# A convolution's norm and Silu ordered ahead of the third head's attention, with the rows of the output projection behind the attention

## The chip, the cores and the metric

The kernel runs on one core of a Trainium2 chip. The metric is the device time of one execution in microseconds (us). A core has TensorE (PE, matmuls; PEld is its weight load), VectorE (DVE), ScalarE (ACT), GpSimd (POOL) and SyncE (SP), which here only issues DMAs. Each engine works its own list of instructions in the order in which they were put down, and waits for others by semaphores.

## The reference

One layer of a streaming encoder, for 512 frames of a new stream and 32 frames of a running one (the sample):

```
mod = silu(c) @ w_ada + b_ada               # shift, scale and gate, twice
h   = x * (1 + sc1) + sh1
z   = h @ w_in + b_in                       # conv value | conv gate | q | k | v
u   = conv_a * sigmoid(conv_b)              # 512 channels
dw  = causal depthwise conv(u), width 31
conv_out = silu(layer_norm(dw))             # norm over the 512 channels
q, k = rope(q), rope(k)                     # 4 heads, two maps of 64 each
p   = softmax of both maps, block-causal in chunks of 64
att = rms_norm((p0 - lam * p1) @ v) * subln_g * (1 - lam_init)    # per head
x   = layer_norm(alpha * x + g1 * (concat(conv_out, att) @ w_out + b_out))
x   = layer_norm(alpha * x + g2 * peer(x * (1 + sc2) + sh2))
```

The last step (peer) selects 16 of 128 x 128 experts for each of 8 heads of a frame and takes up most of the time.

## The kernel before

The program is written with a library that puts the instructions of each engine in order itself: it plays the program on a timing model and sets down, engine by engine, whatever is ready and stands earliest in the text. So the order of the text gives priorities, and the pools of buffers decide what can be ready. The order that comes out is fixed for the chip.

The part that matters here runs from about 145 to 300 us. Eight projection units (`zunit`, two for each head, key then query, 48 matmuls each, line 191) make the keys and queries of a head in two banks of the pool `pa` (function `pat`, two banks in all). ACT adds the bias (line 438), SP swaps halves of 32 rows by four small DMAs (`zw`, line 440), and DVE does the rotation (lines 442 to 445). Then come four attention maps of 128 rows for each head: two score matmuls into a pair of banks (`big`, line 461), maximum on DVE (334), two exponentials on ACT (345), reciprocals, on ACT the first map times its reciprocal (358), on DVE the difference of the two maps (361, into `a`), transposes on PE (467), a copy to `aT` (469), the product with the values (472) and the head's sum of squares and copy on ACT (367, 368). The attention of the sample (`sample_att`) takes all four heads in one map and stands in the text after the fourth head's projection.

The convolution is 124 instructions on DVE, the taps (lines 270 and 273, into `acc`), kept in order by the chain in `conv_taps` and called a few at a time beside the projections and maps (`conv(CB)`, `conv(CZ)`). At the place that `CN` names, the text calls for the rest of them and for `conv_norm`: means by a matmul with ones into two banks of `pa` (376), differences on DVE (379), squares on ACT (383), variances again into two banks of `pa` (385, taken out at 388), root on ACT (389), reciprocal and scaling on DVE (390, 392). With `CN = (3, -1)` that is ahead of the fourth head's attention.

Behind the heads, the Silu of the convolution goes to a buffer `mt` (490, 491), which is split in two parts of reduced precision, `mixh` and `mixl` (492, 493). The heads' outputs are scaled, transposed and split likewise (498 to 510). The output projection (`wgroup`, line 582) multiplies both with the split weights `woh` and `wol` (576, 578), first for tiles 3 and 4, then for tiles 0, 1 and 2. Its rows are prepared by `xload`: b_out times the gate into `bg` (550), and the input rows times alpha plus `bg` (560). Behind it come the query projection and the selection of experts, and then, from about 500 us to the end, the dense products with the expert tables.

Of the kernel before, what the change touches and what calls it, by code (L numbers as in the profile page):

```python
# [8 lines left out]
F32 = mybir.dt.float32  # L9
# [11 lines left out]
NP = 512  # L21
NS = 32
# [38 lines left out]
EXTRA = 8  # L61
RUN = 2
LAST = 4
CN = (3, -1)
CB = 4
CZ = 2
QW = (6, 10, 13)
# [9 lines left out]
def build(tc, I, O):  # L77
# [250 lines left out]
    V.tensor_sub(neglam, lsum[:, 1:2], lsum[:, 0:1])  # L328
    V.tensor_scalar(neglam, neglam, -LAM0, None, op0=OP.add)

    def softmax_parts(parts, ex):
        mx = at.tile([128, 2, 2], F32, tag="mx", name="mx")
        for n, p in enumerate(parts):
            V.tensor_reduce(mx[:, n, :], p, axis=AX.X, op=OP.max)
        nm = at.tile([128, 2], F32, tag="nm", name="nm")
        src = mx[:, 0, :]
        if len(parts) == 2:
            m2 = at.tile([128, 2], F32, tag="m2", name="m2")
            V.tensor_max(m2, mx[:, 0, :], mx[:, 1, :])
            src = m2  # L340
        V.tensor_scalar(nm, src, -0.125, None, op0=OP.mult)
        se = at.tile([128, 2, 2], F32, tag="se", name="se")
        for n, p in enumerate(parts):
            for m in range(2):
                S.activation(ex[n][:, m], p[:, m], AF.Exp, bias=nm[:, m:m + 1], scale=0.125,
                             accum_out=se[:, n, m:m + 1])
        ss = se[:, 0, :]
        if len(parts) == 2:
            s2 = at.tile([128, 2], F32, tag="s2", name="s2")
            V.tensor_add(s2, se[:, 0, :], se[:, 1, :])  # L350
            ss = s2
        rc = at.tile([128, 2], F32, tag="rc", name="rc")
        V.reciprocal(rc, ss)
        rl = at.tile([128, 1], F32, tag="rl", name="rl")
        V.tensor_mul(rl, rc[:, 1:2], neglam)
        out = []
        for n, e in enumerate(ex):
            S.activation(e[:, 0], e[:, 0], AF.Copy, scale=rc[:, 0:1])
            w = e.shape[2]
            a = at.tile([128, 512 if n == 0 else NS], F32, tag=f"a{n}", name="a")  # L360
            V.scalar_tensor_tensor(a[:, :w], e[:, 1], rl, e[:, 0], op0=OP.mult, op1=OP.add)
            out.append(a)
        return out

    def head_out(po, i, h, r):
        sq = at.tile([128, 128], F32, tag="sq", name="sq")
        S.activation(sq[:r], po, AF.Square, accum_out=oms[:r, i, h:h + 1])
        S.copy(otok[:r, i, h, :], po)

    HC = CO // 2  # L370

    def conv_norm():
# [17 lines left out]
        V.reciprocal(crs, crs)  # L390
        for c in range(4):
            V.tensor_mul(acc[:, c], acc[:, c], crs.rearrange("p a b -> p (a b)"))

    pT = [slice(0, 64), slice(64, 128)]
    def sample_att():
# [12 lines left out]
                          tile_position=(64 * m, 32 * h))  # L408
        e = at.tile([128, 2, 512], F32, tag="e", name="e")
        en = at.tile([128, 2, 32], F32, tag="en", name="en", bufs=1)  # L410
        a, an = softmax_parts([sc, sn[:, :, :NS]], [e, en])
        pt = sm()
        for kb in range(4):
            PE.transpose(pt[:, kb * 128:(kb + 1) * 128], a[:, kb * 128:(kb + 1) * 128], ident)
# [14 lines left out]
    for h in range(4):  # L429
# [27 lines left out]
        for i in ((0, 1, 2, 3) if h < 3 else (3, 0, 1, 2)):  # L457
            kl = 128 * (i + 1)
            sc = big()
            for m in range(2):  # L460
                PE.matmul(sc[:, m, :kl], qh[pT[m], i * 128:(i + 1) * 128], kh[pT[m], :kl], start=True, stop=True)
            V.memset(sc[:64, :, kl - 64:kl], NEG)
            e = at.tile([128, 2, 512], F32, tag="e", name="e")
            a, = softmax_parts([sc[:, :, :kl]], [e[:, :, :kl]])
            pt = sm()
            for kb in range(i + 1):
                PE.transpose(pt[:, kb * 128:(kb + 1) * 128], a[:, kb * 128:(kb + 1) * 128], ident)
            aT = at.tile([128, 512], F32, tag="aT", name="aT")
            (V.tensor_copy if h >= 3 else S.copy)(aT[:, :kl], pt[:, :kl])
            po = sm() if h < 3 else pat()  # L470
            for kb in range(i + 1):
                PE.matmul(po[:, :128], aT[:, kb * 128:(kb + 1) * 128], vt[:, kb, h * 128:(h + 1) * 128],
                          start=(kb == 0), stop=(kb == i))
            head_out(po[:, :128], i, h, 128)
            conv(CB)
            if (h, i) == CN:
                conv(124)
                conv_norm()
# [7 lines left out]
    mixh = mixp.tile([128, KC, TM], F32R, name="mixh", bufs=1)  # L486
    mixl = mixp.tile([128, KC, TM], F32R, name="mixl", bufs=1)
    for c in range(4):
        mt = mixp.tile([128, TM], F32, tag="mt", name="mt")
        S.activation(mt[:, :NP], acc[:, c, :NP], AF.Silu, bias=lnb[:, c:c + 1], scale=lng[:, c:c + 1])  # L490
        S.activation(mt[:, NP:], acc[:, c, NP + 30:CO], AF.Silu, bias=lnb[:, c:c + 1], scale=lng[:, c:c + 1])
        V.tensor_copy(mixh[:, c, :], mt)
        V.tensor_sub(mixl[:, c, :], mt, mixh[:, c, :].bitcast(F32))
    for i in (4, 3, 0, 1, 2):
        r = ROWS[i]
        if i in (4, 0):
# [50 lines left out]
    bg = []  # L547
    for s in range(2):
        t = op_.tile([128, D], F32, tag="row", name="bg", bufs=4) if s == 0 else xhB[0]
        V.tensor_mul(t, bo, g1r[s])  # L550
        bg.append(t)
    g1w = rowload(I["ln1_g"])
    b1w = rowload(I["ln1_b"])
# [2 lines left out]
    def xload(i):  # L556
        t = op_.tile([128, D], F32, tag="xp", name="xp", bufs=3) if i < TA else xhB[i - TA]
        r = ROWS[i]
        SY.dma_start(t[:r], I["xtok"][i * 128:i * 128 + r])
        V.scalar_tensor_tensor(t[:r], t[:r], ALPHA, bg[i // 4][:r], op0=OP.mult, op1=OP.add)  # L560
        xps[i] = t

    xload(4)
# [579 lines left out]
```

## Time and profile before

| | us |
|---|---|
| timed runs, median of 3 (lowest to highest) | 1649.08 (1644.37 to 1650.94) |
| the profiled execution | 1638.17 |
| its span, first to last instruction | 1636.4 |
| PE busy | 1567.4 (96%) |
| DVE busy | 1390.4 (85%) |
| ACT busy | 619.1 (38%) |
| POOL busy | 468.4 (29%) |

The times in the rows count from the start of the span. A busy share is an average over stages that differ much, so the rows below are of the stage of the change. The granted clock is the share of full speed at which PE was allowed to run: 1.00 is 2.4 GHz, 0.50 is 1.2 GHz. An idle time in brackets stands ahead of the instruction and names what ended it.

### The profile page before, as it was taken

What the parts mean: (1) busy time and instruction counts of PE and PEld (TensorE: products, weight loads), DVE (VectorE), ACT (ScalarE), POOL (GpSimd) and SP (SyncE); (2) the same over time, 40 slices, a digit from 0 to 9 for tenths busy, and PEclk for the clock granted to TensorE, in tenths of its full rate; (3) what the DMA queues carried; (4) which work ended last, traced back from release to release, by engine and by line L of the source; (5) the groups of instructions that cost most, each with busy time, mean ns of one, the idle gap of its engine ahead of it and who ended that gap; (6) DMA issues with size and microseconds to landing.
All of it is one profiled execution on the core that took longest, in us unless ns stands there. A gap on an engine that the chain in (4) does not pass through costs nothing.

```text
span 1636.4 us, 24735 instructions
## 1 busy us (share of the span) xinstructions
PE 1567.4 (96%) x8911; PEld 1354.1 (83%) x8911; DVE 1390.4 (85%) x2674; ACT 619.1 (38%) x1073; POOL 468.4 (29%) x325
## 2 busy tenths in 40 slices
PE   7999987999988999999999899999999999999996
PEld 4878855786668999999999798888888888888884
DVE  3879987789999999999898668888778778788997
ACT  3312567333122443444454333333333333333332
POOL 0000000000144445247424123533334333244530
PEclk9999987999999999999999999999999999999998
DMA  9776342274478889999999998999999999999993
GB/s 345 286 233 214 86 145 95 77 233 141 140 253 278 293 274 328 342 343 335 367 358 366 372 316 310 347 356 341 352 337 342 328 347 346 336 319 331 338 322 108
DMA packets 184539, 465.59 MB, mean 285 GB/s; under 512 B 17537, under 2 KB 85185, under 8 KB 181217
## 3 DMA queue, kind: packets, MB, share of 16 engines
q1 hardware_dynamic: 138336, 296.23, 52.5%
q0 software_dynamic: 46080, 167.79, 28.9%
q8 instruction: 70, 1.15, 0.3%
q14 instruction: 53, 0.43, 0.1%
HBM read 415.57 MB, written 45.77 MB: 282 GB/s over the span
## 4 chain that ended last, share of the span: by engine, by line
PE 81%; DVE 8%; DMA 5%; issue 3%; ACT 3%; SPq 0%; POOL 0%; DVEq 0%; ACTq 0%
PE acc L994 32%; PE pat L911 30%; PE big L191 3%; PE pat L191 2%; PE pat L685 2%; PE big L826 2%; PE big L582 2%; DMA rowg<-in_u_ji_dram,idx 1%; PE pat L316 1%; PE pat L152 1%; DMA wr<-in_w_ada_dram 1%; DMA raw<-in_uT_dram 1%; DVE jkg L858 1%; DVE s L664 1%; DMA rt<-mod_d 1%
## 5 line engine op out<-in xcount | busy, mean ns | idle before, releaser
L847 POOL DMA_INDIRECT rowg<-in_u_ji_dram,idx x160 | 212.7, 1330 | 789.1 <-DVE VT L661 442.1
L902 DVE TENSOR_TENSOR lo<-raw,hi 128x1024 fp32r<-128x1024 f32 x256 | 311.8, 1220 | 107.4 <-ACT hi L900 101.2
L900 ACT CAST hi<-raw 128x1024 fp32r<-128x1024 f32 x256 | 266.8, 1047 | 307.4 <-PE acc L994 211.8
L847 POOL DMA_INDIRECT rowg<-in_vd_dram,idx x160 | 253.9, 1587 | 328.5 <-DVE accB L869 94.7
L994 PE MATMUL acc<-hi,Pl 128*128 128x512 f32 x768 | 300.8, 392 | 0.0
L994 PE MATMUL acc<-lo,Ph 128*128 128x512 f32 x768 | 281.2, 390 | 0.0
L994 PE MATMUL acc<-hi,Ph 128*128 128x512 f32 x768 | 245.1, 393 | 2.7 <-issue 2.7
L911 PE MATMUL pat<-h2h,hi 128*128 128x384 f32 x1024 | 212.9, 342 | 6.4 <-ACT hi L900 3.3
L911 PE MATMUL pat<-h2h,lo 128*128 128x384 f32 x1024 | 210.3, 342 | 4.8 <-DVE lo L902 4.8
L911 PE MATMUL pat<-h2l,hi 128*128 128x384 f32 x1024 | 210.0, 341 | 0.0
L858 DVE SCALAR_TENSOR_TENSOR jkg<-rowg,xhB 128x1024 f16<-128x1024 f32 x160 | 194.8, 1217 | 10.8 <-DMA rowg<-in_u_ji_dram,idx 8.6
L869 DVE SCALAR_TENSOR_TENSOR accB<-rowg,wB,accB 128x1024 f32<-128x1024 f32 x158 | 201.7, 1277 | 0.5
L911 PEld LDWEIGHTS pat<-h2h,hi 128*128 128x128 f32 x1024 | 181.7, 188 | 13.8 <-ACT hi L900 6.2
L911 PEld LDWEIGHTS pat<-h2h,lo 128*128 128x128 f32 x1024 | 182.2, 188 | 8.3 <-DVE lo L902 5.1
L911 PEld LDWEIGHTS pat<-h2l,hi 128*128 128x128 f32 x1024 | 184.0, 189 | 2.6
L994 PEld LDWEIGHTS acc<-hi,Ph 128*128 128x128 f32 x768 | 144.2, 188 | 30.3 <-issue 3.2
L994 PEld LDWEIGHTS acc<-lo,Ph 128*128 128x128 f32 x768 | 144.1, 188 | 29.1
L994 PEld LDWEIGHTS acc<-hi,Pl 128*128 128x128 f32 x768 | 144.7, 188 | 28.2
L917 ACT ACTIVATE ge<-pat 128x384 f32<-128x384 f32 x128 | 62.6, 491 | 193.5 <-PE pat L911 119.4
L980 ACT CAST Ph<-P 128x384 fp32r<-128x384 f32 x128 | 65.1, 511 | 144.3 <-issue 87.1
L982 DVE TENSOR_TENSOR Pl<-P,Ph 128x384 fp32r<-128x384 f32 x128 | 70.8, 553 | 35.6 <-ACT Ph L980 35.2
L273 DVE SCALAR_TENSOR_TENSOR acc<-U,wdw,acc 128x574 f32<-128x574 f32 x120 | 96.6, 805 | 1.4
(303 smaller groups left out, 1885.6 us busy)
## 6 DMA issues: line engine op xcount, KB each, us to landing
raw<-in_uT_dram SPq DMA_DIRECT2D x128, 512.0 KB
raw<-in_vd_dram SPq DMA_DIRECT2D x128, 512.0 KB
wr<-in_w_ada_dram SPq DMA_DIRECT2D x48, 512.0 KB
g_d<-stg SPq DMA_DIRECT2D x24, 1024.0 KB
gc<-g_d SPq DMA_DIRECT2D x16, 1536.0 KB
wq<-in_w_query_dram SPq DMA_DIRECT2D x32, 512.0 KB
ge_d<-ge SPq DMA_DIRECT2D x70, 192.0 KB
gel<-ge_d SPq DMA_DIRECT2D x70, 192.0 KB
```

Source lines behind the costliest of these rows:

```text
L191: PE.matmul(p[h], a[:, k * 128:(k + 1) * 128], b[:, k, h * HT:(h + 1) * HT], start=(q == 0 and k == 0), stop=(q == 2 and k == KC - 1))
L273: t = V.scalar_tensor_tensor(acc[:, c], U[:, c, w:w + CO], wdw[:, c, w:w + 1], acc[:, c], op0=OP.mult, op1=OP.add)
L847: g = G.indirect_dma_start(out=t, out_offset=None, in_=tab, in_offset=bass.IndirectOffsetOnAxis(ap=idx, axis=0))
L858: V.scalar_tensor_tensor(jk, t, 1.0, h2B[s], op0=OP.mult, op1=OP.mult, accum_out=aB[s][:, q:q + 1])
L869: V.scalar_tensor_tensor(ac, t, w[:, q - c0:q - c0 + 1], ac, op0=OP.mult, op1=OP.add)
L900: S.copy(hi, raw)
L902: V.tensor_sub(lo, raw, hi.bitcast(F32))
L911: mm = PE.matmul(p[:, :NA], a[:, k * 128:(k + 1) * 128], b[:, k, :], start=(n == 0), stop=(n == 23))
L917: S.activation(ge, p[:, :NA], AF.Gelu)
L980: S.copy(Ph, Pf)
L982: V.tensor_sub(Pl, Pf, Ph.bitcast(F32))
L994: mm = PE.matmul(accs[i][hf], a[:, sl], b[:, hs], start=(j == 0 and n == 0), stop=(j == NK - 1 and n == 2))
```

## The change

Three edits. `CN` becomes `(2, -1)`, so that the rest of the taps and `conv_norm` stand in the text ahead of the third head's attention, and the Silu is done in place in `conv_norm` instead of after the heads. The first product and sums of the rows for the output projection are put behind the last map's difference on DVE by a dependency that only orders them. For the 512 frames the first map is no longer multiplied by its reciprocal: the second map's factor takes in the first map's sum, and the reciprocal comes in as a scale where ACT takes the head's output out of PSUM. The sample's map is done as before.

```
-CN = (3, -1)
+CN = (2, -1)
...
+    MAPS = []
+
+    def after_maps(t):
+        tc.add_manual_dep(t.ins, MAPS[-1].ins.name, ORD, reason="behind the attention on this engine")
+
+    def softmax_parts(parts, ex, norm):
...
-        V.tensor_mul(rl, rc[:, 1:2], neglam)
+        if norm:
+            V.tensor_mul(rl, rc[:, 1:2], neglam)
+        else:
+            V.scalar_tensor_tensor(rl, ss[:, 0:1], rc[:, 1:2], neglam, op0=OP.mult, op1=OP.mult)
...
-            S.activation(e[:, 0], e[:, 0], AF.Copy, scale=rc[:, 0:1])
+            if norm:
+                S.activation(e[:, 0], e[:, 0], AF.Copy, scale=rc[:, 0:1])
...
-            V.scalar_tensor_tensor(a[:, :w], e[:, 1], rl, e[:, 0], op0=OP.mult, op1=OP.add)
+            MAPS.append(V.scalar_tensor_tensor(a[:, :w], e[:, 1], rl, e[:, 0], op0=OP.mult, op1=OP.add))
...
-        S.activation(sq[:r], po, AF.Square, accum_out=oms[:r, i, h:h + 1])
-        S.copy(otok[:r, i, h, :], po)
+        S.activation(sq[:r], po, AF.Square, scale=rs, accum_out=oms[:r, i, h:h + 1])
+        if r == 128:
+            S.activation(otok[:r, i, h, :], po, AF.Copy, scale=rs)
+        else:
+            S.copy(otok[:r, i, h, :], po)
...
             V.tensor_mul(acc[:, c], acc[:, c], crs.rearrange("p a b -> p (a b)"))
+            S.activation(acc[:, c], acc[:, c], AF.Silu, bias=lnb[:, c:c + 1], scale=lng[:, c:c + 1])
...
-        mt = mixp.tile([128, TM], F32, tag="mt", name="mt")
-        S.activation(mt[:, :NP], acc[:, c, :NP], AF.Silu, bias=lnb[:, c:c + 1], scale=lng[:, c:c + 1])
-        S.activation(mt[:, NP:], acc[:, c, NP + 30:CO], AF.Silu, bias=lnb[:, c:c + 1], scale=lng[:, c:c + 1])
-        V.tensor_copy(mixh[:, c, :], mt)
-        V.tensor_sub(mixl[:, c, :], mt, mixh[:, c, :].bitcast(F32))
+        for o, n, a0 in ((0, NP, 0), (NP, NS, NP + 30)):
+            src = acc[:, c, a0:a0 + n]
+            V.tensor_copy(mixh[:, c, o:o + n], src)
+            V.tensor_sub(mixl[:, c, o:o + n], src, mixh[:, c, o:o + n].bitcast(F32))
...
-        V.tensor_mul(t, bo, g1r[s])
+        after_maps(V.tensor_mul(t, bo, g1r[s]))
...
-        V.scalar_tensor_tensor(t[:r], t[:r], ALPHA, bg[i // 4][:r], op0=OP.mult, op1=OP.add)
+        after_maps(V.scalar_tensor_tensor(t[:r], t[:r], ALPHA, bg[i // 4][:r], op0=OP.mult, op1=OP.add))
```

The order that comes out changes at three places. The first is PE around the fourth head's projection (line 191; 461 is scores, 467 transposes, 472 the product with the values, 376 and 385 the norm's means and variances). Before, the end of that projection stands among the third head's maps, ahead of the means:

```order
L472 MATMUL sm<-vt,aT 128x128 x2
L467 MATMUL sm<-ident,a 128x128 x3
L191 MATMUL pat<-hl,wh 128x272 x2
L461 MATMUL big<-qk 128x256 x2
L472 MATMUL sm<-vt,aT 128x128 x3
L461 MATMUL big<-qk 128x384 x2
L467 MATMUL sm<-ident,a 128x128 x4
L376 MATMUL pat<-acc,ones_c 128x287 x6
```

Now, from the variances on (397; 480 and 485 are transposes and products with the values, 420 the sample's scores):

```order
L420 MATMUL big<-ks,qs 32x32 x6
L485 MATMUL sm<-vt,aT 128x128 x3
L397 MATMUL pat<-csq,ones_c 128x287 x4
L480 MATMUL sm<-ident,a 128x128 x4
L397 MATMUL pat<-csq,ones_c 128x287 x4
L485 MATMUL sm<-vt,aT 128x128 x4
L191 MATMUL pat<-hh,wh 128x272 x8
L191 MATMUL pat<-hh,wl 128x272 x8
L191 MATMUL pat<-hl,wh 128x272
L191 MATMUL pat<-hh,wh 128x272 x8
L191 MATMUL pat<-hh,wl 128x272 x8
L191 MATMUL pat<-hl,wh 128x272 x15
```

The fourth head's projection (96 matmuls; the second unit's 48 follow without anything between) has moved behind the norm's last matmul, and behind it stand only the last scores of the sample and the fourth head's maps.

The second place is DVE at the last tap (273). Before, the rows for the output projection (550, 560) and the fourth head's rotation (443, 445) stand between the taps:

```order
L550 TENSOR_TENSOR bg<-rt,row 128x1024
L353 RECIPROCAL rc<-se 128x2
L341 TENSOR_SCALAR nm<-mx 128x2
L273 SCALAR_TENSOR_TENSOR acc<-U,wdw,acc 128x574
L560 SCALAR_TENSOR_TENSOR xp<-xp,bg 128x1024
L355 TENSOR_TENSOR rl<-rc,neglam 128x1
L560 SCALAR_TENSOR_TENSOR xp<-xp,bg 128x1024
L462 MEMSET big 64x2x64
L273 SCALAR_TENSOR_TENSOR acc<-U,wdw,acc 128x574
L443 TENSOR_TENSOR zw<-zw,sinT 128x544
```

Now the last tap is followed by the norm (391 differences, 400 variances taken out, 402 reciprocal, 404 scaling) and only then by the fourth head's rotation (455 to 458):

```order
L273 SCALAR_TENSOR_TENSOR acc<-U,wdw,acc 128x574
L391 TENSOR_TENSOR acc<-acc,pat 128x287 x8
L358 RECIPROCAL rc<-se 128x2
L363 SCALAR_TENSOR_TENSOR rl<-se,rc,neglam 128x1
L370 SCALAR_TENSOR_TENSOR a<-e,rl 128x512
L400 TENSOR_SCALAR crs<-pat 128x287 x2
L402 RECIPROCAL crs<-crs 128x574
L404 TENSOR_TENSOR acc<-acc,crs 128x574 x4
L455 TENSOR_TENSOR t_2517<-z,cosT 128x544
L456 TENSOR_TENSOR zw<-zw,sinT 128x544
```

What stood between the taps has gone behind them, and one map's difference (370) is all that the third head still has to do there.

The third place is DVE at the end of the attention. Before, the norm's last steps (390, 392) stand among the fourth head's maps (361 difference, 469 copy of the transposed map):

```order
L390 RECIPROCAL crs<-crs 128x574
L469 COPY aT<-sm 128x512
L361 SCALAR_TENSOR_TENSOR a<-e,rl 128x256
L341 TENSOR_SCALAR nm<-mx 128x2
L469 COPY aT<-sm 128x128
L392 TENSOR_TENSOR acc<-acc,crs 128x574 x4
L469 COPY aT<-sm 128x256
```

Now the rows (562, 572) stand there (370 and 482 are the difference and the copy):

```order
L370 SCALAR_TENSOR_TENSOR a<-e,rl 128x384
L482 COPY aT<-sm 128x256
L562 TENSOR_TENSOR bg<-rt,row 128x1024
L510 TENSOR_SCALAR oms<-oms 128x8
L482 COPY aT<-sm 128x384
L572 SCALAR_TENSOR_TENSOR xp<-xp,bg 128x1024 x3
```

The product for the rows stands ahead of the last copy, the three sums behind it.

## Rows read from the trace of the kernel before

**Rows 1.** Stretch, us, busy (count) by engine, granted clock, DMA share, GB/s.

```profile
800.00:1636.00 836.00, 814.72 (x4102) 714.32 (x4099) 677.18 (x866) 306.26 (x444) 292.97 (x218) 0.99 0.94 330
```

**Rows 2.** Chain that ended last, in order of time: start us, us, what.

```profile
153.56 6.22 PE pat L191 x47
...
211.76 5.18 DMA rt<-mod_d
...
216.96 9.21 DMA xp<-in_xtok_dram
...
269.29 8.39 PE big L582 x24
```

**Rows 3.** Same columns as rows 1, stretches of 5 us.

```profile
200.00:205.00 5.00, 5.00 (x37) 4.10 (x36) 4.73 (x12) 3.81 (x12) 0.00 (x0) 1.00 0.18 43
...
225.00:230.00 5.00, 1.91 (x6) 1.22 (x6) 4.87 (x10) 1.57 (x6) 0.00 (x0) 0.50 0.56 223
...
270.00:275.00 5.00, 5.00 (x14) 2.93 (x13) 4.54 (x8) 3.30 (x5) 0.00 (x0) 0.51 0.81 329
275.00:280.00 5.00, 5.00 (x27) 3.54 (x26) 3.39 (x6) 2.32 (x3) 0.00 (x0) 1.00 0.00 0
```

**Rows 4.** Timeline of DVE: start us, us, instruction, count [idle before <-releaser].

```profile
219.01 1.23 DVE L550 TENSOR_TENSOR bg<-rt,row 128x1024 f32<-128x1024 f32 x1 [0.95 <-DMA row<-mod_d]
...
222.91 1.23 DVE L560 SCALAR_TENSOR_TENSOR xp<-xp,bg 128x1024 f32<-128x1024 f32 x1 [0.62 <-DMA xp<-in_xtok_dram]
...
228.47 0.81 DVE L273 SCALAR_TENSOR_TENSOR acc<-U,wdw,acc 128x574 f32<-128x574 f32 x1
229.19 0.72 DVE L445 TENSOR_TENSOR qk<-t,zw 128x544 f32<-128x544 f32 x1
...
232.18 1.23 DVE L334 TENSOR_REDUCE mx<-big 128x2 f32<-128x1024 f32 x1 [0.88 <-PE big L405]
...
234.24 0.81 DVE L273 SCALAR_TENSOR_TENSOR acc<-U,wdw,acc 128x574 f32<-128x574 f32 x1
...
236.47 2.99 DVE L379 TENSOR_TENSOR acc<-acc,pat 128x287 f32<-128x287 f32 x8 [0.41 <-PE pat L376]
...
245.99 0.81 DVE L388 TENSOR_SCALAR crs<-pat 128x287 f32<-128x287 f32 x2
```

**Rows 5.** Timeline of PE.

```profile
230.21 1.92 PE L405 MATMUL big<-wr,qs 64*32 64x512 f32 x4 [1.73 <-ACT qs L446]
...
235.10 2.28 PE L376 MATMUL pat<-acc,ones_c 128*128 128x287 f32 x4
...
243.57 2.21 PE L385 MATMUL pat<-csq,ones_c 128*128 128x287 f32 x8
```

**Rows 6.** Timeline of ACT.

```profile
159.81 0.87 ACT L438 ACTIVATE z<-pat,vec 128x272 f32<-128x272 f32 x2 [4.98 <-PE pat L191]
...
229.94 0.22 ACT L446 COPY qs<-qk 128x32 f32<-128x32 f32 x1 [0.90 <-DVE qk L445]
...
242.67 1.25 ACT L383 ACTIVATE csq<-acc 128x574 f32<-128x574 f32 x2
```

**Rows 7.** Timeline of DVE: swapped halves awaited; last transposed map copied.

```profile
165.54 0.73 DVE L443 TENSOR_TENSOR zw<-zw,sinT 128x544 f32<-128x544 f32 x1 [1.49 <-DMA zw<-z]
...
265.42 0.55 DVE L469 COPY aT<-sm 128x384 f32<-128x384 f32 x1
```

**Rows 8.** DVE by line, 236 to 269: busy us, mean ns | idle.

```profile
L334 DVE TENSOR_REDUCE mx<-big 128x2 f32<-128x1024 f32 (+3 forms) x4 | 3.3, 822 | 0.1
...
L361 DVE SCALAR_TENSOR_TENSOR a<-e,rl 128x512 f32<-128x512 f32 (+3 forms) x5 | 2.9, 584 | 0.4 <-ACT e L358 0.4
L493 DVE TENSOR_TENSOR mixl<-mt,mixh 128x544 fp32r<-128x544 f32 x4 | 2.8, 708 | 0.0
```

**Rows 9.** Groups by line, ACT, 227 to 269 us.

```profile
L345 ACT ACTIVATE e<-big,nm 128x512 f32<-128x512 f32 (+3 forms) x12 | 6.9, 577 | 0.5 <-DVE nm L341 0.3
...
L345 ACT ACTIVATION_READ_ACCUMULATOR e<-big,nm 128x1 f32 x12 | 2.4, 198 | 0.0
```

More of the change, by code (lines that the diff above doesn't have):

```diff
@@ L329, in build @@
     V.tensor_scalar(neglam, neglam, -LAM0, None, op0=OP.add)
-    def softmax_parts(parts, ex):
+    MAPS = []
+    def after_maps(t):
+        tc.add_manual_dep(t.ins, MAPS[-1].ins.name, ORD, reason="behind the attention on this engine")
+    def softmax_parts(parts, ex, norm):
         mx = at.tile([128, 2, 2], F32, tag="mx", name="mx")
@@ L351, in softmax_parts, with head_out @@
             ss = s2
-        rc = at.tile([128, 2], F32, tag="rc", name="rc")
+        rc = at.tile([128, 2], F32, tag="rc", name="rc", bufs=4)
         V.reciprocal(rc, ss)
         rl = at.tile([128, 1], F32, tag="rl", name="rl")
-        V.tensor_mul(rl, rc[:, 1:2], neglam)
+        if norm:
+            V.tensor_mul(rl, rc[:, 1:2], neglam)
+        else:
+            V.scalar_tensor_tensor(rl, ss[:, 0:1], rc[:, 1:2], neglam, op0=OP.mult, op1=OP.mult)
         out = []
         for n, e in enumerate(ex):
-            S.activation(e[:, 0], e[:, 0], AF.Copy, scale=rc[:, 0:1])
+            if norm:
+                S.activation(e[:, 0], e[:, 0], AF.Copy, scale=rc[:, 0:1])
             w = e.shape[2]
             a = at.tile([128, 512 if n == 0 else NS], F32, tag=f"a{n}", name="a")
-            V.scalar_tensor_tensor(a[:, :w], e[:, 1], rl, e[:, 0], op0=OP.mult, op1=OP.add)
+            MAPS.append(V.scalar_tensor_tensor(a[:, :w], e[:, 1], rl, e[:, 0], op0=OP.mult, op1=OP.add))
             out.append(a)
-        return out
-    def head_out(po, i, h, r):
+        return out, rc[:, 0:1]
+    def head_out(po, i, h, r, rs=1.0):
         sq = at.tile([128, 128], F32, tag="sq", name="sq")
-        S.activation(sq[:r], po, AF.Square, accum_out=oms[:r, i, h:h + 1])
-        S.copy(otok[:r, i, h, :], po)
+        S.activation(sq[:r], po, AF.Square, scale=rs, accum_out=oms[:r, i, h:h + 1])
[3 more added lines that the diff above has]
+            S.copy(otok[:r, i, h, :], po)
     HC = CO // 2
@@ L410, in sample_att @@
         en = at.tile([128, 2, 32], F32, tag="en", name="en", bufs=1)
-        a, an = softmax_parts([sc, sn[:, :, :NS]], [e, en])
+        (a, an), _ = softmax_parts([sc, sn[:, :, :NS]], [e, en], True)
         pt = sm()
@@ L463, in build @@
             e = at.tile([128, 2, 512], F32, tag="e", name="e")
-            a, = softmax_parts([sc[:, :, :kl]], [e[:, :, :kl]])
+            (a,), rs = softmax_parts([sc[:, :, :kl]], [e[:, :, :kl]], False)
             pt = sm()
@@ L473, in build @@
                           start=(kb == 0), stop=(kb == i))
-            head_out(po[:, :128], i, h, 128)
+            head_out(po[:, :128], i, h, 128, rs)
             conv(CB)
```

## The prediction

> **What bounds the kernel now.** I read the page first: PE is busy 96% of the span. From 800 us to the end PE works 814.72 of 836 us at a granted clock of 0.99 [rows 1], so whatever makes the work before it late makes the end late by as much. The change touches the part from about 180 to 300 us, so the second view is the chain of waits there [rows 2]. It runs through the projection units of the heads (one unit is 6.22 us of PE), then, after the last unit, through two DMAs of rows for the output projection (5.18 and 9.21 us), and reaches the first matmul of the output projection at 269.29. That start is the mark which I forecast; behind it the order of all engines is the same but for small swaps, so I carry its shift to the end one to one.
>
> The third view is the stretches of 5 us [rows 3]. At 200 us PE (5.00 of 5) and DVE (4.73 of 5) are both full: projections on the one, taps of the convolution on the other. At 225 us DVE is still full (4.87) while PE does 1.91 and has fallen to 0.50, the 1.2 GHz level. The timeline of DVE [rows 4] shows what it does until its last tap at 234.24, and what it waited for in between: 0.95 and 0.62 us for rows of the output projection, 0.88 us for the scores of the sample.
>
> **The change part by part.** All three edits meet in one place: which work stands between the last tap and the output projection, and what runs beside it. The order shows that the fourth head's projection moves behind the norm: it takes its two banks from the same pool of two as the means and variances of the norm, and these are now asked for first. (The norm itself doesn't come ahead of the third head's maps: it needs the last tap, and three of the four maps stand before that.)
>
> *The last tap comes earlier.* DVE starts an instruction some 0.09 before the one ahead ends (228.47 + 0.81 against 229.19 [rows 4]). What leaves the stretch ahead of the last tap: the fourth head's rotation, 6 instructions at 0.72 - 0.08, 3.8; one product and three sums for the output projection's rows, 4 at 1.15, 4.6; their waits, 1.6; the two maxima of the sample, 1.3, and their wait, 0.9. Together 12.2. The last tap ended at 234.24 + 0.81 = 235.05, so now at about 222.9. The maps of heads two and three now follow each other faster on DVE; each still has its score matmul and exponentials done a microsecond or more before DVE comes to it, so I add no stall here.
>
> *The norm up to the release of its banks.* Before, from 235.05 to 245.99 + 0.81 = 246.80 [rows 4], 11.75 us, with the fourth head's and the sample's work in between: the upper bound. Alone it is 1.42 to the first difference (236.47 - 235.05), 2.99 for the eight differences, 1.25 for the last two squares [rows 6], 2.21 for the last variances [rows 5], 0.81 for taking them out [rows 4]: 8.7. I take 8.7, since the fourth head's maps are no longer there. The projection can start at 231.6.
>
> *The fourth head's projection, now bare.* Two units at 6.22 and the gap of half a microsecond between them [rows 2]: 12.9. PE was sparse for long before it, as at 225 us, so I expect it at 0.50 when it begins. The output projection shows what that costs: it begins at 269.29 [rows 2], the stretch from 270 is granted 0.51 and the next 1.00 [rows 3]; 5.4 us at half rate lose 2.7. So 12.9 to 15.6; I take 15.6, end 247.2. DVE has meanwhile only the end of the norm, ACT the Silu, and both wait for the rest.
>
> The Trainium skill (Perfetto Trace Analysis, Optimization Strategy) says that where the most contended engine changes over time, interleaving the stretches may help. It speaks against this change, which takes the PE stretch out of the DVE stretch, and the 5.00 beside 4.73 at 200 us [rows 3] agree that the two had run together. By that rule alone the 15.6 would come on top in full, 1664.7; by the rows part of it is given back below.
>
> *Swap and rotation.* From the start of a unit's bias step to the multiplication that needs its swapped halves: 159.81 [rows 6] to 165.54 [rows 7], 5.7, with a wait for the DMA. Then two steps at 0.64 and 0.72 and the copy of the sample's queries, 1.6 in all. On SP the four swap DMAs of the query unit now stand behind two row loads of 512 KB, so the bound above is the 9.21 that a DMA behind such loads took [rows 2]. I take 5.7, as the loads ahead are two and not five. Queries of the sample ready at 254.5; before it was 229.94 + 0.22 = 230.16 [rows 6]. So far 24.3 us later.
>
> *From there to the output projection.* Before 39.1 (230.16 to 269.29), with differences, reciprocal, scaling, Silu and the split of the convolution between the maps. Now only the maps are left, and I add their chain up: scores until DVE takes the maximum 2.0 (230.21 [rows 5] to 232.18 [rows 4]); the maximum 1.3; second halves of the split that stand before the next step, 2.5 (four tiles at 0.71 [rows 8], their first piece done during the scores); two small ones 0.3; the sample's exponentials 2.0 (two wide ones and two narrow, 0.58 + 0.20 in the mean [rows 9]); its normalisation and difference 1.9; maximum of the first map of the fourth head 1.4; its exponentials 1.6. Then DVE's list to its last transposed map: four differences of maps at 0.50, two maxima at 0.74 [rows 8], three copies at about 0.4, the product for the rows 1.15, ten small ones together 0.9, a wait of 0.6 for the last exponentials: 7.4. From that copy to the first output matmul 3.9, as before (265.42 [rows 7] to 269.29 [rows 2]). Sum 24.3. Bounds: 22 if the waits between engines overlap better, 27 if of the old 39.1 only the instructions of the norm and the Silu drop out. I take 24.3: start at 278.8.
>
> *Edits with no price of their own.* Sixteen passes on ACT go away, but ACT isn't what the maps wait for while DVE is full; in the tail the passes of the fourth head are already left out of my sum. The scale in the head's output steps costs about 0.1 on ACT, and only the last one is seen. The three row sums (3.5 us on DVE) that now come right behind the last copy lie beside the first output matmuls at half rate, which need the split's second piece only after some 4 us; without that cover they would cost up to 1.
>
> *Sum.* 222.9 + 8.7 + 15.6 + 7.3 + 24.3 = 278.8 against 269.29: 9.5 us later. The profiled execution took 1638.17 (span 1636.4); it would take 1647.7. The timed runs had a median of 1649.08, 11 us above that execution, so on their scale I forecast 1658.6.
>
> **The rivals.**
> *The clock holds (no change).* If the maps of heads two and three, now denser, keep PE at 1.00, then the half-rate losses vanish: 2.7 in the projection, about 0.8 in the means (2.28 us for four [rows 5] against 2.21 for eight), some 2 in scores and maps (1.92 for the four of the sample [rows 5]), and 2.7 at the start of the output projection, which before it paid. That is 8.2 of the 9.5: 1650.4. It decides if PE is still granted 1.00 when the block begins at 231. For it: at 200 us the clock is 1.00. Against: there the projections filled PE, and just these are gone; at 225 us, without them, it was 0.50 [rows 3].
> *Nothing is given back (slower still).* The swap lands behind the row loads (9.21 instead of 5.7) and the tail only drops to 27: 3.5 and 2.7 more, +15.7, 1664.8. For it: the chain shows exactly such a wait in this place. Against: fewer loads stand ahead.
> *The shift doesn't reach the end.* If DMA binds the last 800 us (share 0.94 [rows 1]), the loads of the tables could run on while the output projection is late. Then 1649 to 1652. Against: PE is at 97% there, and the loads wait for buffers that PE frees.
>
> **How the numbers follow.** Forecast 0.56, its own range +3 to +16 us; clock holds 0.20; nothing given back 0.16; not carried to the end 0.08. About 0.5%, 8.2 us, is what a measurement of this kernel can tell from no change. Six in ten of the forecast's own range lie above that, 0.34, and the slower rival adds 0.16: slower 0.50. Of the rest the forecast gives 0.19 to no change, the first and third rival 0.25: 0.44. 0.06 stays for faster, which needs the clock to hold and every bound at its low end. The range from 1646 to 1667 runs from just under the two cases near no change to just over the slower rival.
>
> **What would show it.** In the profile after: the last tap ends near 223; 96 projection matmuls in one block on PE from about 232 to 247 with DVE mostly idle beside the second half; the copy of the sample's queries near 254; the first output matmul near 279, 24 us behind that copy instead of 39; PE at 0.50 somewhere between 205 and 235. Wrong it is if the block begins before 228 or runs at 1.00 from its start, if the tail is shorter than 21 us, or if the output projection is late and the end is not.

## The result, and the profile after

The changed kernel takes 1659.93 us (median of 11 runs, 1653.62 to 1665.32), the kernel before 1645.62 (11 runs, 1638.36 to 1652.97). The ratio, estimated from all these runs, is 1.0079, 95% interval 1.0061 to 1.0097: 13 us slower, 10 to 16 (the two medians alone lie 14.3 apart). Forecast was 9.5 slower; that the forecast time, 1658.6, is so near the median is partly luck, since it was built on a median of 1649.08 for the kernel before. The execution profiled after took 1661.77 (span 1660.0).

The chain of waits of the changed kernel (start us, us, what), which answers [rows 2]:

```profile
223.28 1.74 PE pat L388 x4
...
227.14 0.99 PE sm L485 x6
228.13 1.94 PE pat L397 x8
...
230.51 1.94 PE pat L397 x8
232.45 0.89 PE sm L485 x8
233.34 5.93 PE pat L191 x47
...
239.84 6.35 PE pat L191 x48
...
248.94 6.18 DMA zw<-z
...
263.03 1.28 ACT L350
...
284.93 6.46 PE big L594 x20
```

Read it from the top: means (L388), variances (L397) with map matmuls of the third head between them (L485), then both projection units of the fourth head (L191), one behind the other, then the DMA that swaps its halves, and at last a table load of ScalarE. The kernel before had the units beside the taps, and no swap of the fourth head between the last tap and the output projection. The first matmul of the output projection starts at 284.93, 15.6 us later than at 269.29 [rows 2]. The stretches of 5 us, with the columns of [rows 3]:

```profile
225.00:230.00 5.00, 4.65 (x35) 3.71 (x34) 3.14 (x9) 3.66 (x10) 0.00 (x0) 0.77 0.00 0
230.00:235.00 5.00, 5.00 (x36) 4.58 (x35) 2.21 (x3) 4.44 (x8) 0.00 (x0) 1.00 0.02 3
...
250.00:255.00 5.00, 0.00 (x0) 0.00 (x0) 0.00 (x0) 0.00 (x0) 0.00 (x0) 0.62 1.00 259
255.00:260.00 5.00, 2.03 (x8) 0.57 (x8) 4.62 (x12) 0.22 (x1) 0.00 (x0) 0.50 0.80 320
...
270.00:275.00 5.00, 4.89 (x31) 3.31 (x31) 3.59 (x14) 3.42 (x17) 0.00 (x0) 0.83 0.16 61
275.00:280.00 5.00, 4.96 (x39) 3.81 (x38) 4.08 (x13) 3.57 (x18) 0.00 (x0) 1.00 0.36 85
...
285.00:290.00 5.00, 5.00 (x15) 3.16 (x16) 4.20 (x9) 1.99 (x3) 0.00 (x0) 0.66 0.04 16
```

From 250 to 255 no engine does anything and the DMA engines are busy all the time (share 1.00): PE, VectorE and ScalarE all wait for the swap. The projection ran at 1.00, the full clock; the half rate, 0.50, came behind it. The timeline, with the columns of [rows 4], first of the other engines and then of SP's queue:

```profile
222.43 0.80 DVE L273 SCALAR_TENSOR_TENSOR acc<-U,wdw,acc 128x574 f32<-128x574 f32 x1
...
246.08 0.87 ACT L451 ACTIVATE z<-pat,vec 128x272 f32<-128x272 f32 x2 [0.19 <-PE pat L191]
...
255.24 0.73 DVE L456 TENSOR_TENSOR zw<-zw,sinT 128x544 f32<-128x544 f32 x1 [7.53 <-DMA zw<-z]
...
256.76 0.22 ACT L459 COPY qs<-qk 128x32 f32<-128x32 f32 x1 [9.81 <-DVE qk L458]
...
263.03 1.28 ACT L350 ACT_TABLE_LOAD   x1 [6.05 <-DVE nm L346]
264.33 0.69 ACT L350 ACTIVATE e<-big,nm 128x512 f32<-128x512 f32 x1
...
270.16 2.65 PE L437 MATMUL pat<-wr,aT 128*32 128x128 f32 x16
...
281.15 0.55 DVE L482 COPY aT<-sm 128x384 f32<-128x384 f32 x1
...
284.93 0.91 PE L594 MATMUL big<-woh,mixh 128*128 128x512 f32 x2 [2.18 <-ACT woh L588]
```

```profile
246.20 0.33 SPq L553 DMA_DIRECT2D rt<-in_b_out_dram  x1
246.58 0.44 SPq L553 DMA_DIRECT2D rt<-mod_d  x1
247.12 2.42 SPq L453 DMA_DIRECT2D zw<-z  x4
```

The last tap ends at 223.23. The queries' four swap DMAs (L453) are issued behind two row loads (L553) and land 8 us after the first of them is issued; from the bias step (L451) to the multiplication of the swapped halves (L456) it is 9.16 us; the sample's queries are copied at 256.98; 27.95 us later (the tail) the output projection begins.

Is the shift carried to the end? One and the same piece of the chain, of the kernel before and then of the changed one:

```profile
751.08 7.11 PE pat L911 x40
```

```profile
766.04 7.11 PE pat L923 x40
...
785.44 10.09 POOL rowg L859
```

At 751 it is 15.0 us. Some 7 us more come in around a gather of table rows at 785 to 815 of this execution, far from the change; the spans differ by 23.6, the medians by 14.3. What the timed runs say on this stands under the experiments.

### The profile page after: what moved, and what is told of

Its sections match the earlier page's. It is cut to its first block, busy times and chain, and to the rows that moved or that the text cites. A ratio compares the mean times of both kernels' runs of the same rounds, so it can differ in the third digit from the quotient of the medians.

```text
span 1660.0 us, 24735 instructions
## 1 busy us (share of the span) xinstructions
PE 1574.5 (95%) x8911; PEld 1359.7 (82%) x8911; DVE 1392.5 (84%) x2682; ACT 611.3 (37%) x1051; POOL 487.0 (29%) x325
## 4 chain that ended last, share of the span: by engine, by line
PE 79%; DVE 10%; DMA 4%; issue 3%; ACT 2%; POOL 1%; SPq 0%; DVEq 0%; ACTq 0%; POOLq 0%
PE acc L1006 32%; PE pat L923 28%; PE big L191 3%; PE pat L191 2%; PE pat L697 2%; PE big L594 2%; PE big L838 2%; PE pat L152 1%; PE pat L316 1%; DVE jkg L870 1%; DMA raw<-in_uT_dram 1%; DVE s L676 1%; DMA rowg<-in_u_ji_dram,idx 1%; DVE IT L674 1%; DVE IT L678 1%
## 5 line engine op out<-in xcount | busy, mean ns | idle before, releaser
L859 POOL DMA_INDIRECT rowg<-in_u_ji_dram,idx x160 | 206.5, 1291 | 809.9 <-DVE VT L673 458.1
L859 POOL DMA_INDIRECT rowg<-in_vd_dram,idx x160 | 278.8, 1742 | 312.7 <-DVE accB L881 92.5
L923 PEld LDWEIGHTS pat<-h2h,lo 128*128 128x128 f32 x1024 | 184.1, 190 | 13.8 <-DVE lo L914 10.8
```

The lines of the kernel that those rows point to most:

```text
L859: g = G.indirect_dma_start(out=t, out_offset=None, in_=tab, in_offset=bass.IndirectOffsetOnAxis(ap=idx, axis=0))
L923: mm = PE.matmul(p[:, :NA], a[:, k * 128:(k + 1) * 128], b[:, k, :], start=(n == 0), stop=(n == 23))
```

## The experiments

Marks of each profiled execution (us), and the time as a ratio to the kernel before, from runs on the same chip:

| kernel | last tap ends | sample's queries ready | first output matmul | ratio (95% interval) |
|---|---|---|---|---|
| before | 235.05 | 230.16 | 269.29 | 1 |
| changed | 223.23 | 256.98 | 284.93 | 1.0079 (1.0061 to 1.0097) |
| order_only | 219.94 | 255.92 | 290.71 | 1.0136 (1.0114 to 1.0159) |
| order_undone | 231.51 | 223.62 | 269.77 | 1.0012 (0.9995 to 1.0028) |
| own_banks | 225.88 | 222.85 | 284.26 | 1.0076 (1.0059 to 1.0094) |
| proj_ahead | 228.41 | 221.60 | 263.16 | 0.9975 (0.9966 to 0.9984) |
| swap_first | 221.44 | 250.00 | 277.48 | 1.0063 (1.0047 to 1.0079) |
| exp_early | 221.63 | 255.16 | 281.20 | 1.0097 (1.0080 to 1.0115) |
| woh_first | 224.15 | 258.55 | 285.64 | 1.0104 (1.0088 to 1.0120) |
| rows_free | 222.33 | 255.55 | 287.26 | 1.0106 (1.0092 to 1.0121) |
| warm | 221.10 | 253.78 | 295.05 | 1.0187 (1.0172 to 1.0202) |
| warm20 | 223.07 | 257.42 | 285.01 | 1.0101 (1.0086 to 1.0117) |
| old_order_tuned | 228.03 | 219.03 | 263.78 | 0.9974 (0.9960 to 0.9987) |
| proj_ahead_woh | 228.98 | 222.17 | 263.73 | 0.9969 (0.9955 to 0.9982) |

The last column follows the one ahead of it: 21.4 us at the output projection are 22.3 in the time, 0.5 are 2.0, 25.8 are 30.7, and 6.1 early are 4.1 saved. All 13 agree within 5 us, 11 of them within 3. So within that scatter the shift reaches the end. Differences of two or three us between kernels measured beside different runs of the kernel before (the changed kernel and the later ones) are read from the stretch in the trace, not from the ratio. That matters for the small edits: exp_early (1.0097), woh_first (1.0104) and warm20 (1.0101) don't lie below the changed kernel's 1.0079, so no timed run shows that they save anything. Several ratios also lie above the range expected for them: order_only (up to 1.012), order_undone (1.001), exp_early and woh_first (1.008), warm20 (1.009) and above all warm (1.007).

**The order alone (order_only), and all but the order (order_undone).**

```diff
 # order_only, in the kernel before
-CN = (3, -1)
+CN = (2, -1)
 # order_undone, in the changed kernel
-CN = (2, -1)
+CN = (3, -1)
```

> The kernel before with one number changed: the norm of the convolution is asked for ahead of the third head's maps. Silu stays behind the loop, the rows' products and sums stay where the scheduler puts them, every map is normalised on ScalarE.
> Theory A (the order alone makes the change slower, since the fourth head's projection waits for the norm's two banks): 1.005 to 1.012 of the kernel before, the block of 96 projection matmuls begins on PE after the last tap (between 230 and 245), and the first output matmul stands 10 to 22 us later than 269.29.
> Rival B (Silu ahead, the rows behind the maps or the unnormalised map make it slower): within 0.3% of the kernel before.

> The changed kernel with the norm back behind the third head's maps; Silu right behind the norm, the rows behind the maps and the unnormalised first map stay.
> Theory A: the loss is gone: 0.996 to 1.001 of the kernel before (16 passes less on ScalarE and 3.5 us of row sums out of VectorE's full stretch can only give a few us), first output matmul between 265 and 270.
> Rival B: 1.004 or more, since what costs is still in it.

One number makes 1.0136, and without it the other edits change nothing that can be measured. order_only is above the changed kernel too: in the new order the other edits give something back: 5.8 us at the output projection. Rival B falls.

**Other banks for the norm (own_banks).**

```diff
-        pm = [pat() for _ in range(2)]
+        pmb = big()
+        pm = [pmb[:, h, :] for h in range(2)]
...
-        pv = [pat() for _ in range(2)]
+        pvb = big()
+        pv = [pvb[:, h, :] for h in range(2)]
```

> The changed kernel, but the means and the variances of the norm take one double bank each from the pool of the scores instead of two single banks each from the pool of the projections; so the fourth head's projection waits for nothing of the norm, though the norm is asked for ahead of it as in the changed kernel.
> Theory A (the wait for the banks is the cause): the projection lies beside the taps again, the last tap ends near 227 (222.9 and the fourth head's rotation, 3.8), the first output matmul stands near 263 to 268, and the time is 0.993 to 0.999 of the kernel before.
> Rival C (the loss comes from the norm and its split standing ahead of the maps on VectorE, whichever banks it takes): the first output matmul stands at 275 or later, 1.004 or more.

The projection went back beside the taps (193.0 to 212.5) and the last tap ended at 225.88, but the output projection was as late as in the changed kernel (284.26 against 284.93), as rival C has it. The timeline of PE shows why the test was not clean:

```profile
225.93 4.89 PE L389 MATMUL big<-acc,ones_c 128*128 128x287 f32 x10 [10.11 <-DVE acc L273]
...
234.58 0.49 PE L476 MATMUL big<-qk 64*128 64x128 f32 x4
...
244.16 2.08 PE L476 MATMUL big<-qk 64*128 64x512 f32 x4 [4.28 <-ACT e L350]
```

Now the score matmuls of the third head (L476) stand behind the norm, because their banks are the ones it holds; PE sat idle for 10.11 us, until the last tap, with the means first in its queue and those scores behind them. The wait had only moved to another pool. So the request had to be moved and not the bank.

**The projection asked for first (proj_ahead).**

```diff
-    for h in range(4):
+    def project(h):
         qk = [None, None]
...
+        return qk
...
+    heads = {}
+    for h in range(4):
+        if h not in heads:
+            heads[h] = project(h)
+        if (h, -1) == CN:
+            heads[h + 1] = project(h + 1)
+        qh, kh = heads[h]
```

> The changed kernel with one thing moved: the fourth head's projection is written ahead of the norm, so it takes its two banks before the norm asks for them; the norm is still asked for ahead of the third head's maps, and its banks are the same two.
> Theory A (the projection's wait behind the norm's banks is the cause): 0.997 to 1.002 of the kernel before, the projection beside the taps (PE between 200 and 232), the first output matmul 266 to 272.
> Rival C (the norm ahead of the maps is the cause, whoever has the banks): 1.005 or more, first output matmul 278 or later.

Better than theory A had it: first output matmul at 263.16, below the 266 to 272 expected, and faster than the kernel before. On PE:

```profile
203.62 1.27 PE L191 MATMUL pat<-hh,wh 128*128 128x272 f32 x8
...
208.69 1.67 PE L191 MATMUL pat<-hl,wh 128*128 128x272 f32 x12
...
216.51 1.13 PE L482 MATMUL big<-qk 64*128 64x512 f32 x4
...
228.46 1.92 PE L388 MATMUL pat<-acc,ones_c 128*128 128x287 f32 x4
```

The fourth head's units lie beside the taps, the third head's last scores stand at 216.51 (own_banks: 244.16), and the norm is still asked for ahead of the maps. Rival C falls: not the norm ahead of the maps is the cause, but the projection behind the norm. The Trainium skill (Perfetto Trace Analysis, Optimization Strategy) holds that stretches with different contended engines may gain from interleaving; the two orders, 263.16 against 284.93, agree.

**The swap and the loads on its queue (swap_first).**

```diff
-                SY.dma_start(zw[32 * r:32 * r + 32], z[32 * (r ^ 1):32 * (r ^ 1) + 32])
+                SWAPS.append(SY.dma_start(zw[32 * r:32 * r + 32], z[32 * (r ^ 1):32 * (r ^ 1) + 32]))
...
-        SY.dma_start(t, bcast_rows(src, 128))
+        d = SY.dma_start(t, bcast_rows(src, 128))
+        tc.add_manual_dep(d.ins, SWAPS[-1].ins.name, ORD, ...)
...
-        SY.dma_start(t[:r], I["xtok"][i * 128:i * 128 + r])
+        d = SY.dma_start(t[:r], I["xtok"][i * 128:i * 128 + r])
+        tc.add_manual_dep(d.ins, SWAPS[-1].ins.name, ORD, ...)
```

> The changed kernel with the loads of rows (bias and modulation rows and the rows of x) ordered behind the last of the swap DMAs of the fourth head's queries on SP's queue; nothing else is edited.
> Theory D (the swap is late because it stands behind two row loads of 512 KB on its queue): from the bias step to the multiplication of the swapped halves 5 to 5.7 us instead of 9.16, the first output matmul 3.5 us earlier than 284.93, time 1.004 to 1.007 of the kernel before.
> Rival E (what makes it late are the loads that run beside it, ahead of or behind it in the queue): still 8 to 10 us, and 1.007 to 1.009 as in the changed kernel.

```profile
243.28 0.86 ACT L452 ACTIVATE z<-pat,vec 128x272 f32<-128x272 f32 x2 [0.20 <-PE pat L191]
...
248.27 0.73 DVE L457 TENSOR_TENSOR zw<-zw,sinT 128x544 f32<-128x544 f32 x1 [3.36 <-DMA zw<-z]
```

From the bias step to the multiplication 4.99 us, where the changed kernel took 9.16 (246.08 to 255.24). The loads still run right behind the swap, and don't slow it. Theory D holds: it is what is ahead in the queue. The first output matmul moved by 7.5, more than the 4.2 of the swap: 1.8 was there at the last tap already, 1.0 lies in the norm (8.87 us from the last tap to the first projection matmul, 9.87 in the changed kernel) and 0.5 in the tail, from the copy of the sample's queries on.

**The table load (exp_early), and the weights' casts ahead of the square root (woh_first).**

```diff
 # exp_early, behind the Silu loop of conv_norm ("last" is its last activation)
+        pre = cp.tile([128, 1], F32, name="pre")
+        V.memset(pre, 0.0)
+        p = S.activation(pre, pre, AF.Exp)
+        tc.add_manual_dep(p.ins, last.ins.name, ORD, ...)
 # woh_first, in wgroup (SQ holds the square root of the heads' norm)
-                S.copy(hi, raw)
+                cw = S.copy(hi, raw)
+                if tiles[0] == 3 and kk == 0:
+                    tc.add_manual_dep(SQ[0].ins, cw.ins.name, ORD, ...)
```

> The changed kernel with one exponential of a single column (of a tile of zeros that nothing reads) on ScalarE right behind the last Silu, so the function table is changed there.
> Theory F (the table load of 1.28 us lies on the path since it waits with its exponential for the sample's maximum): from the copy of the sample's queries to the first output matmul 26.6 to 26.8 us instead of 27.95; the time 1.006 to 1.008 of the kernel before, since 1.3 us are a tenth of a per cent.
> Rival G (the load only fills a wait; the scores of the fourth head or VectorE end last there): 27.7 to 28.2.

> The changed kernel with the square root of the heads' norm on ScalarE (and its table load) ordered behind the first two casts of the output projection's weights.
> Theory H (the load, the square root and the last head's two output steps, 2.1 us, stand on ScalarE ahead of the cast that the first output matmul waits for): from the copy of the sample's queries to the first output matmul 25.8 to 26.6 us instead of 27.95, time 1.006 to 1.008.
> Rival I (the late square root delays the attention's half of the output projection by as much as the start gains): the first output matmul is earlier, but the end of the first output group isn't.

ScalarE in exp_early:

```profile
240.93 1.28 ACT L408 ACT_TABLE_LOAD   x1
242.22 0.20 ACT L408 ACTIVATE pre<-pre 128x1 f32<-128x1 f32 x1
254.94 0.22 ACT L463 COPY qs<-qk 128x32 f32<-128x32 f32 x1 [9.50 <-DVE qk L462]
261.23 0.69 ACT L350 ACTIVATE e<-big,nm 128x512 f32<-128x512 f32 x1 [6.07 <-DVE nm L346]
...
267.06 1.93 PE L441 MATMUL pat<-wr,aT 128*32 128x128 f32 x16 [0.26 <-ACT aT L433]
```

The first exponential of the sample stands 6.07 us behind the queries and no longer 7.35 (264.33 - 256.98): 1.28 gone, the whole load. The tail is 26.04, shorter by another 0.6, and that is PE's clock: the sample's first sixteen products with the values (L441) ran 1.93 us at a granted 1.00, in the changed kernel 2.65 at 0.71 (L437), and the scores behind them came 0.72 earlier still. In six other executions with the norm ahead of the third head's maps (order_only, swap_first, exp_early, woh_first, rows_free, warm20) they took 1.93 to 2.19; the changed kernel's is the slowest, and whether that belongs to the kernel or to this one execution no run shows. It has to be taken off before its tail is compared with another. Theory F holds for the load; rival G falls. The Trainium skill (ScalarE: Activation LUTs, What ACT_TABLE_LOAD costs) puts the load at 1.28 us and a drain at 1.38 more, 2.66 for every switch; here only the 1.28 show, the activation starting 0.01 to 0.02 behind the load, and the measurement decides.

In woh_first, on PE, the same sixteen products:

```profile
271.73 1.94 PE L437 MATMUL pat<-wr,aT 128*32 128x128 f32 x16
```

Its tail is 27.09, 0.86 shorter. But 0.61 of that is there at the last copy of a transposed map, ahead of which nothing was edited: it is the products above, 1.94 instead of 2.65. The edit itself gives 0.25 (3.53 from that copy to the first output matmul, 3.78 in the changed kernel), far less than theory H had. The first transposed piece of the normalised result behind the output projection (L631, in the changed kernel L628) is taken out at 330.23, 44.6 behind the first output matmul; in the changed kernel it is 44.15. So more than the 0.25 is given back there, as rival I has it, and theory H falls.

**The rows left to the scheduler (rows_free).**

```diff
     def after_maps(t):
-        tc.add_manual_dep(t.ins, MAPS[-1].ins.name, ORD, ...)
+        pass
```

> The changed kernel without the rule that puts the products and sums of the rows behind the maps; the scheduler may place them where it did before.
> Theory N (of what the changed kernel has over the order alone, 21.4 against 15.6 us at the first output matmul, most is these four instructions of 1.15 to 1.2 us out of the stretch between the sample's queries and the last map): from the copy of the queries to the first output matmul 31.5 to 33.5 us, time 1.010 to 1.012 of the kernel before.
> Rival O (the unnormalised first map, which takes four passes off ScalarE between a map's exponentials and its difference, and the early Silu make it): 27.5 to 29.5, 1.007 to 1.009.

VectorE, inside the tail:

```profile
259.29 1.22 DVE L572 SCALAR_TENSOR_TENSOR xp<-xp,bg 128x1024 f32<-128x1024 f32 x1
...
263.14 1.22 DVE L572 SCALAR_TENSOR_TENSOR xp<-xp,bg 128x1024 f32<-128x1024 f32 x1
264.45 1.22 DVE L572 SCALAR_TENSOR_TENSOR xp<-xp,bg 128x1024 f32<-128x1024 f32 x1
```

The three sums stand between the sample's queries and its exponentials again; the tail is 31.71, 3.8 longer, and 4.5 with the sixteen products at one rate (1.93 here, 2.65 in the changed kernel). Theory N holds. Of the 6.8 by which order_only's tail (34.79; its products took 1.94) is longer than the changed kernel's, 3.8 are the rows (4.5, less the 0.7 of those products) and 3.1 the unnormalised map and the early Silu together, which no run here tells apart. Part is given back at once: the first transposed piece of the normalised result (L628) is taken out at 329.69, in the changed kernel at 329.08.

**PE kept busy during the wait (warm, warm20).**

```diff
+    def warm(n):
+        pw = pat()
+        for _ in range(n):
+            PE.matmul(pw[:, :HC], ones_c, U[:, 0, 0:HC], start=True, stop=True)
...
         if h == 3:
+            warm(40)     # 20 in warm20
             sample_att()
...
+        warm(24)         # in warm alone, behind the sample's scores
```

> The changed kernel with 64 matmuls more, of 128 x 287 like the norm's, whose results nothing reads: 40 on PE behind the fourth head's projection, while it waits for the swap, and 24 behind the sample's scores.
> Theory L (the half rate that PE is granted from 255 to 270 costs in the tail what the prediction had charged to the projection): PE granted 1.00 there, from the copy of the sample's queries to the first output matmul 25.5 to 26.5 us instead of 27.95, and the first output group shorter by 1 to 2 us as well; time 1.005 to 1.007 of the kernel before.
> Rival M (PE's rate isn't on that path, VectorE and ScalarE are): 27.5 to 28.3 though PE is granted 1.00.

> The changed kernel with 20 matmuls of 128 x 287 behind the fourth head's projection, whose results nothing reads; one takes 0.49 us at 1.00 (two records of 0.245 each), so 9.8 us of the 10.8 in which PE waits for the swap, and nothing behind the sample's scores. The order of the other work is the changed kernel's, but for the sample's two maxima, which stand on VectorE behind the split and not inside it.
> Theory L (PE's half rate from 255 to 270 costs in the tail what the prediction had charged to the projection): PE granted 1.00 while the sample's scores run, 25.5 to 27 us from the copy of the sample's queries to the first output matmul instead of 27.95.
> Rival M (VectorE and ScalarE end last there at either rate): 27.5 to 28.5 though PE is granted 1.00.
> Both expect 1.006 to 1.009 of the kernel before; so the stretch decides and not the time.

The first try was my error of size. Each of these matmuls leaves two records; I took one record's 0.245 us for the matmul. So 40 took 19.60 us and held the sample's scores up by 9. The second fits. PE in its stretches, and one line of its timeline:

```profile
255.00:260.00 5.00, 2.69 (x15) 1.30 (x13) 4.18 (x13) 0.22 (x1) 0.00 (x0) 1.00 0.79 274
260.00:265.00 5.00, 0.00 (x0) 0.00 (x0) 3.45 (x10) 1.39 (x2) 0.00 (x0) 0.60 0.67 220
265.00:270.00 5.00, 3.57 (x13) 1.92 (x13) 2.31 (x7) 2.81 (x10) 0.00 (x0) 0.50 0.98 401
```

```profile
257.47 1.06 PE L423 MATMUL big<-wr,qs 64*32 64x512 f32 x4 [0.89 <-ACT qs L464]
```

The scores ran at 1.00 (1.06 us, in the changed kernel 1.93), and the tail is 27.59 against 27.95. Rival M holds for the scores: VectorE splits the convolution meanwhile and wouldn't come to them sooner, and the exponential's table load began 6.18 us behind the queries, no earlier than the changed kernel's 6.05. PE then idled for almost 8 us (258.58 to 266.39) and was at 0.50 from 265 on as before, so what the half rate costs from there to 270 stays open. Behind it theory L has a small part: the 0.36 come from the sixteen products again (2.18 instead of 2.65), which as exp_early shows are on the path.

**Two tries at something faster (old_order_tuned, proj_ahead_woh).** The first is order_undone with Silu behind the loop and the edits of swap_first and woh_first; the second is proj_ahead with that of woh_first.

> The changed kernel with the norm back behind the third head's maps, Silu back behind the loop, the loads of rows behind the last swap DMA on SP's queue and the first two casts of the output projection's weights ahead of the square root of the heads' norm; the unnormalised first map and the rows behind the maps stay. A try at a version faster than both.
> Theory J (waits that the traces show on the path are worth their length): two table loads of 1.28 us fewer ahead of the output projection than with Silu right behind the norm, VectorE's wait of 2.4 us for the swap gone: first output matmul 263 to 267, 0.995 to 0.999 of the kernel before.
> Rival K (VectorE is full until the last tap and sets the start whatever waits go): 268 to 271, within 0.2%.

> The kernel with the fourth head's projection written ahead of the norm, and in it the first two casts of the output projection's weights ahead of the square root of the heads' norm on ScalarE. A try at a version faster still.
> Theory P (with the attention late by nothing else, the casts end last there: they begin at 262.06, 5.2 us behind the last Silu): first output matmul 260 to 262 instead of 263.16, time 0.995 to 0.997 of the kernel before.
> Rival Q (as in the changed kernel, where the same edit moved the first matmul 0.9 us and the end of the first output group by nothing): within 0.1% of 0.9975.

Theory J's times came true, 263.78 and 0.9974; its terms did so in part. VectorE's wait of 2.44 us for the swap (order_undone) is gone, and 3.5 of the 6.0 us over order_undone are there at the last tap. But ahead of the first output matmul stand three table loads from the norm on, in order_undone four: one fewer and not two. What brings the other 2.5 no run separates. Theory P falls: the first output matmul didn't come earlier than in proj_ahead (263.73 against 263.16). PE and ScalarE there:

```profile
258.96 2.84 PE L493 MATMUL pat<-vt,aT 128*128 128x128 f32 x10 [1.78 <-DVE aT L490]
...
262.25 0.36 ACT L378 ACTIVATE otok<-pat,rc 128x128 f32<-128x128 f32 x1
262.64 1.99 ACT L597 CAST woh<-wr 128x1024 fp32r<-128x1024 f32 x2
```

The cast still stands behind the last map's output step, which waits for PE and that for VectorE's copies. The three faster kernels (0.9969 to 0.9975) can't be told apart; each is 4 to 5 us faster than the kernel before, and some 17 faster than the changed one.

## Why the prediction was right, and where its size was off

The direction and its reason held: the projection, taken out from beside the taps, is what costs (order_only, order_undone, proj_ahead). By the prediction's own steps:

| step | forecast | measured | off by |
|---|---|---|---|
| last tap ends | 222.9 | 223.23 | +0.3 |
| norm until the projection starts | 8.7 | 9.9 (to 233.10) | +1.2 |
| projection | 15.6 | 13.1 (to 246.2) | -2.5 |
| swap, rotation, copy of the queries | 7.3 | 10.8 (to 256.98) | +3.5 |
| tail to the first output matmul | 24.3 | 27.95 (to 284.93) | +3.65 |
| shift at the first output matmul | 9.5 | 15.6 | +6.1 |

*The norm.* I dropped all map matmuls from it, but only the fourth head's were gone. Three pieces of the third head's, 0.99, 0.44 and 0.89, are in the chain of after. That it is only 1.2 is since the first difference began 0.87 behind the last tap and not 1.42: the four matmuls of the means took 1.74, before 2.28 [rows 5].

*The projection.* The 2.7 for a half-rate start was wrong. PE was granted 0.77 from 225 and 1.00 from 230: the variances and the third head's maps kept it at work just ahead of the block, where the kernel before was at 0.50 [rows 3]. "Runs at 1.00 from its start" stood in the prediction's own list of what would make it wrong. It was also the condition set for the rival in which the clock holds. That rival's other savings weren't there: PE was at 0.50 for the scores and part of the maps, and at 0.66 at the start of the output projection.

*The swap.* I took 5.7, "as the loads ahead are two and not five". The count was right and the inference wrong: two loads ahead made it 9.16, and with none it is 4.99. The upper bound, 9.21 [rows 2], was the right row; that it comes so near is luck, since it is one larger transfer and not four small ones.

*The tail.* 1.28 is the exponential's table load. Before, Silu came behind the exponentials of the sample; now it stands ahead of them, so the function changes back at a place where VectorE and PE wait for it, and I had no term for that. Another 2.15 are in the list from the fourth head's first exponentials to the last copy: 9.55 us from 271.60 to 281.15, of which VectorE works 8.10, where I had 6.8 of work and 0.6 of waiting. The work that I missed is small: thirteen instructions of 0.15 to 0.22 us, for which I had ten with 0.9 together. Of the waiting some 0.6 is PE's late clock in this execution (see woh_first). The last 0.3 is spread ahead of the list. The end, 3.9 from the last copy, came out at 3.8.

So the shift at the first output matmul, 15.6, is the slower rival's 15.7 and not my 9.5. That rival had the swap right by its mechanism, row loads ahead of it. Its tail of 27 is near 27.95 in size alone: what made it long is a table load, small instructions and PE's clock. The unhidden projection, the forecast's reason, held, and the good clock of the other rival took 2.5 back. That the time, 13 us, lies below the shift in the trace, and that the median fell so near the forecast time, is partly luck. That the shift might not reach the end is refuted by the table of marks. The unpriced edits were not free either way: in the new order they are worth 5.8 us at the output projection, in the old one nothing.

## What to carry to other kernels

Where buffers are handed out in the order of the program's text, asking early for work that can't start yet makes later work that could run wait for it: ask for the runnable work first, and check what else uses the pool (own_banks moved the wait, proj_ahead removed it). When a small transfer is on the path, read what its queue issues just ahead of it, and bound it by a row with such loads ahead, however few. When an activation of another function is moved ahead of a wait, count the table load behind it where the others wait.

## What was not expected of the hardware

A table load of ScalarE may or may not run ahead in a wait. In the changed kernel it was idle for 6.05 us before the exponential's load at 263.03, which started only when the operand was there, and a tiny exponential put early takes it out (1.28). In the same execution the Silu's load ran while its operand was still awaited:

```profile
234.29 1.28 ACT L405 ACT_TABLE_LOAD   x1
...
238.27 0.87 ACT L405 ACTIVATE acc<-acc,vec 128x574 f32<-128x574 f32 x1 [2.70 <-DVE acc L404]
```

What decides between the two no run here shows, so read the order of load and wait from the trace. Loads issued behind a small transfer on the same queue didn't slow it (4.99 us), while two loads ahead of it nearly doubled its time (9.16).
